# Strassen pairs of a conv-FFN: tokens normalized ahead of the split, four products in one PSUM bank, squares added in pairs

## The chip, the cores and the metric

The kernel runs on one core of a Trainium2 chip. The metric is the time of one execution in device microseconds. The core has a matrix engine (TensorE, PE), which multiplies a 128 x 128 stationary tile by a moving tile and writes to PSUM, and three engines for elementwise work: VectorE (DVE), ScalarE (ACT) and GpSimd (POOL). SyncE (SP) issues the DMAs. Each engine has its own list of instructions; semaphores join them.

## What is computed

One layer of a streaming encoder for 2080 tokens of width 1024 (2048 of a prompt, 32 of a running stream), in float32. The core of the reference:

```python
def rmsnorm(x, g):
    y = x32 * lax.rsqrt(jnp.mean(x32 * x32, axis=-1, keepdims=True) + NORM_EPS)
    return (y * g.astype(jnp.float32)).astype(x.dtype)

def conv_ffn(h, conv_prev, p):
    gu = h @ p['w_up']
    gate, up = gu[..., :D_FF], gu[..., D_FF:]
    gate_c, conv_new = causal_dwconv(gate, conv_prev, p['ffn_conv_w'], p['ffn_conv_b'])
    act = jax.nn.gelu(gate_c, approximate=True) * up
    return act @ p['w_down'], conv_new

def layer(x, ...):
    m, ... = mixer(rmsnorm(x, p['g_mix_pre']), ...)
    x = x + rmsnorm(m, p['g_mix_post'])
    f, ffn_conv_new = conv_ffn(rmsnorm(x, p['g_ffn_pre']), ffn_conv_prev, p)
    x = x + rmsnorm(f, p['g_ffn_post'])
```

The mixer is stick-breaking attention beside a state-space scan, with one input and one output projection. D_FF is 2816, so w_up makes 22 tiles of gate and 22 of up, each of 128 columns.

## The kernel before

**Layout.** Activations lie with features on the partitions and tokens along the free axis. The tokens are taken in four blocks s = 0 to 3 of 512, 512, 512 and 544. Every float32 factor is split into a high part (a copy rounded to float32r, made by ACT) and a low part (the rest, a subtract on POOL or DVE), and each product of tiles is three matmuls: high x high, high x low, low x high (`dense`, L145). So `part` (L1052) and `divide` (L130) are the split of an activation and of a weight tile.

**Order.** A first phase makes projections and the scan for all blocks. Then `build` runs attention for block s+1 (`Attention.heads`) with the rest of block s as its filler (`Tail.stream`, L1365): a Python generator whose steps `heads` draws between attention's own slots. For block 3 no attention is left; its stream runs alone, after `alone` (L1430) has given it more PSUM banks and more places for weights. The order in which the generators emit is the starting point; a planner that simulates time (`schedule_with_timeline_sim=True`) sets each engine's list from it, with one exception: `pin` (L69) ties the first matmul of a unit to the last one marked before, so that in blocks 0 to 2 PE keeps the emitted order of units, attention's scores and transposes among them. In block 3 pinning is off.

**The stream of a block** takes its tokens in two halves, a and b. `owed` is what is left of the block before: its last two downs, of which 8 steps go first. Then come

1. `out_units` of half a: the output projection, eight units of 24 matmuls;
2. `out_units` of half b, with `residual` and `ready` of half a emitted between its steps;
3. `residual` of half b;
4. in blocks 1 to 3 `squares`, `far`, the rest of `owed`, the root of half b, and two early pairs;
5. the pairs (or, in block 0, `up`), in groups of three or two, with `finish` of the block before and `down` of the last group between them.

`residual` (L991) makes h = x + rmsnorm(m): the root of mean squares of m by `rstd_narrow`, a multiply (L1010), the add (L1015, DVE and POOL in turn), a store of h (`hS`), and in blocks 1 to 3 the multiply by the gain (L1018, ACT), into m. `squares` (L1058) then squares h in place, which has to wait for the store.

`rstd_steps` (L182) is the root: matmuls with a column of ones (L193) sum the squares over the partitions, one output column for 128 tokens, one for each tile in `sq`, eight tiles in `root` (L1041); then a multiply-add on DVE, a power on POOL, and a matmul with the identity (L228) that spreads the result over the partitions as r.

**Strassen.** Blocks 1 to 3 compute gate and up of both token halves in seven products in place of eight (the Winograd form). `near` (L1062) splits half a, `far` (L1071) splits half b and makes three sums of tiles with their splits (`put`), X[6], X[7] and X[4]; `self.X` names the seven activations. Weight sums were made by block 0 and lie in DRAM (`sS`). The tokens are split **without** their root r: `pair` (L1142) multiplies the gate by r as it evicts it (L1180 on DVE, L1184 on POOL), and up stays unscaled, since the norm behind the down removes a scale of each token; `rcol` keeps what this does to its epsilon.

A pair (a gate tile and an up tile) is seven products of 12 matmuls of 256 columns (272 in block 3). Four PSUM banks are used: 1 and then 2 in one, 5 and 3, 6 and 7, and 4. Each bank is read where its first product is complete:

```python
        for i in (1, 2, 5, 6, 3, 7, 4) if j < AHEAD else (1, 5, 6, 2, 3, 7, 4):
            w = self.factor(s, j, i)
            base = {2: 1, 3: 5, 7: 6}.get(i, i)
            if base == i:
                ps[i] = self.bank()
```

ACT copies 1 (L1174) and 5 (L1176); DVE evicts 6, 3, 7 and 4 with an add (L1157) and 2 with r (L1180). Then follow the convolution over tokens (L1201, L1203), GELU (L1207 to L1210), the product with up (L1211), and the split into `ah` and `al` (L1216, L1217), which `down` (L1292) multiplies. The first two pairs (`AHEAD`) are early: their products 1 and 2 need half a only.

`factor` (L1115) fetches a weight: 1, 2 and 4 come split from DRAM (`wS_up`), the others come whole (`sS`, four `wraw` buffers) and are split by ACT (L135) and POOL (L136). In block 3 `slot` turns through ten places; elsewhere a ring of six (`w`) serves pairs and downs. `bank` turns through three banks (five in block 3). `finish` (L1330) is the last norm of the block before, its residual add and the store of y.

Of the kernel before, what the change touches and what calls it, by code (L numbers as in the profile page):

```python
# [20 lines left out]
RBUFS = 4  # L21
FAST = (1, 2, 3)
AHEAD = 2

# [38 lines left out]
class Kernel:  # L63
# [54 lines left out]
    def held(self, pool, tag):  # L118

        return pool.tile([P, 2, self.unit, P], F32R, name=tag or "w", bufs=1 if tag else self.wbufs)  # L120
# [810 lines left out]
class Tail:  # L931
# [7 lines left out]
    def __init__(self, kn, att, ctx, pu):  # L939
# [14 lines left out]
        self.raws, self.n, self.n_bank = {}, 0, 0  # L954
# [36 lines left out]
    def residual(self, s, half):  # L991
# [8 lines left out]
        self.h = []  # L1000
        for c in range(KC):
            m = self.m(c, half)
            if self.late:
                x = self.late.tile([P, 272], F32, name="xr", bufs=8)[:, :n]
            else:
                if c % 2 == 0:
                    pair = self.yp.tile([P, 548], F32, name="gb") if c % 4 else self.yp.tile([P, 546], F32, name="y")
                x = pair[:, 272 * (c % 2) : 272 * (c % 2) + n]
# [5 lines left out]
            h = x if fast else m  # L1014
            eng.tensor_tensor(h, m, x, op=ALU.add)  # L1015
            nc.sync.dma_start(kn.hS[s][:, c, c0:c1], h)
            if fast:
                nc.scalar.activation(m, h, AF.Copy, scale=kn.col(C_GFFN + c))  # L1018
            else:
                nc.scalar.activation(x, m, AF.Square)  # L1020
            self.h.append(x)
            yield

# [17 lines left out]
    def root(self, s, half, pin=False):  # L1041
        kn, nc, att = self.kn, self.kn.nc, self.att
        c0, c1 = half
        if c0 == 0:
# [4 lines left out]
            att.tmp, *kn.bank, self.h, c1 - c0, D, out=self.r[:, c0:c1], rcol=col, pin=pin  # L1049
# [8 lines left out]
    def squares(self):  # L1058
        for h in self.h:
            self.kn.nc.scalar.activation(h, h, AF.Square)  # L1060

    def near(self, s, half):  # L1062

        kn, nc = self.kn, self.kn.nc
        c0, c1 = half
        hi, lo = self.x = self.cat
        for k in range(KC):
            self.part(self.m(k, half), hi[k][:, c0:c1], lo[k][:, c0:c1], nc.vector if k % 2 else None)
            yield

    def far(self, s, half):  # L1071
# [24 lines left out]
        for k in two:  # L1096
            sub(b21, b22, b21, k)
# [17 lines left out]
    def factor(self, s, j, i):  # L1115


        kn = self.kn
        if i in (1, 2, 4):
            key = ("up", NJ + j if i == 4 else j, 4 * (i > 1))  # L1120
            return kn.recall(self.ring(), [key], 4, self.slot())
        return kn.divide(self.ring(), kn.raw(self.raws[j, i][:], 4), 4, None, self.slot())

    def ring(self):

        return self.keep or self.kn.wp

    def slot(self):

        if not self.keep:  # L1130
            return None
        self.n += 1
        return f"w{self.n % 10 // 2}{self.n % 2 * 4}"

    def bank(self):

        self.n_bank += 1
        k = max(self.n_bank, 0) % (5 if self.keep else 3)
        pool, name = self.pu if k >= (3 if self.keep else 2) else self.po
        return pool.tile([P, 512], F32, name=name)  # L1140

    def pair(self, s, j, acts):  # L1142
# [16 lines left out]
        for i in (1, 2, 5, 6, 3, 7, 4) if j < AHEAD else (1, 5, 6, 2, 3, 7, 4):  # L1159
            w = self.factor(s, j, i)  # L1160
            base = {2: 1, 3: 5, 7: 6}.get(i, i)
            if base == i:
                ps[i] = self.bank()
            b = ps[base]
            for k in (0, 2):
                kn.dense(
                    b, w[k : k + 2], self.X[i], 0, h, k0=k, first=base == i and k == 0, last=base != i and k == 2,
# [9 lines left out]
            elif i == 6:  # L1177
                add(t, b, p1)
            elif i == 2:
                nc.vector.tensor_tensor(gb[:, 2 : 2 + h], b, self.r[:, :h], op=ALU.mult)  # L1180
# [406 lines left out]
```

## Time and profile before

| | |
|---|---|
| median of 3 runs | 2983.7 us (2981.67 to 2986.89) |
| profiled execution | 2982.5 us |
| its span, first to last instruction | 2980.7 us |
| mean granted TensorE clock | 0.969 |
| DMA | 632.97 MB, mean 212 GB/s |

How to read the rows: in a row of instructions stand line, engine, operation, output<-inputs, the shape, the count, then busy time in us, mean ns of one, and the idle time of the engine just before them with what ended most of it. In a row by windows stand the window, its width, the busy time of PE, PE's weight loads, DVE, ACT and POOL (counts in brackets), the granted clock, the share of the DMA engines and GB/s. In a row of waits stand who waited, for whom, us in total, times, and the longest. In a timeline row stand start, duration, engine, line, operation and count, with idle time and its releaser in square brackets. A float32 matmul of one column is recorded as two. Tile names: `o`, `u`, `t` are PSUM banks, `n` the quarters of the tokens and their sums, `gb`, `y`, `ub` and `xr` work tiles.

### The profile page before, as it was taken

The page shows a single profiled execution, that of the slowest core. Times are in us where ns is not written, and L with a number is a line of the kernel's source. Part 1 is how long each engine was busy: PE and PEld are TensorE (multiplying, and loading weights), DVE is VectorE, ACT ScalarE, POOL GpSimd, SP SyncE. Part 2 cuts the span into 40 slices and gives each one's busy share as a digit, 9 for nine tenths or more (in the row PEclk, how much of TensorE's full clock was granted, in tenths as well). Part 3 has the DMA queues.
Part 4 walks back from the last instruction along what each step waited for, and adds up shares of the span by engine and source line. Part 5 has one row for each costly group of instructions (what it writes and reads, how often), then busy time and mean ns, then how long its engine had stood idle before and what let it go on. Part 6 is the DMA issues. An engine that isn't in the chain of part 4 may idle for free. (4 is left out here: it accounts for less than half of the span.)

```text
span 2980.7 us, 51672 instructions
## 1 busy us (share of the span) xinstructions
PE 2791.3 (94%) x18307; PEld 2485.9 (83%) x18307; DVE 1947.4 (65%) x2920; ACT 1464.4 (49%) x3075; POOL 1770.3 (59%) x1552
## 2 busy tenths in 40 slices
PE   7999999989899999999899999998999999789997
PEld 6777778877787778778788999987998989789997
DVE  7666576557675667746867667688577763744554
ACT  4344444337655445446655555666455544433322
POOL 4555565435756666645866666577666655855645
PEclk9999999989999999999899999999999999899998
DMA  5646463658687778786576667756666666666664
GB/s 177 181 152 174 149 177 122 160 150 286 230 273 262 263 268 284 273 285 230 168 242 206 213 214 244 265 166 209 214 209 209 206 229 213 210 205 210 203 222 140
DMA packets 371139, 632.97 MB, mean 212 GB/s; under 512 B 77531, under 2 KB 196963, under 8 KB 370883
## 3 DMA queue, kind: packets, MB, share of 16 engines
q1 hardware_dynamic: 370882, 629.67, 65.1%
q8 instruction: 146, 2.39, 0.3%
q14 instruction: 111, 0.90, 0.1%
HBM read 480.31 MB, written 149.23 MB: 211 GB/s over the span
## 5 line engine op out<-in xcount | busy, mean ns | idle before, releaser
L136 POOL TENSOR_TENSOR w<-wraw,w 128x512 fp32r<-128x512 f32 (+3 forms) x508 | 768.1, 1520 | 401.3 <-ACT w L135 372.4
L151 PE MATMUL o<-xhi,w 128*128 128x256 f32 (+2 forms) x3776 | 923.1, 328 | 28.8 <-ACT xhi L324 8.0
L151 PEld LDWEIGHTS o<-xhi,w 128*128 128x128 f32 x3776 | 653.8, 193 | 95.3 <-ACT xhi L324 8.0
L151 PE MATMUL o<-xlo,w 128*128 128x256 f32 (+2 forms) x1888 | 617.6, 327 | 5.9 <-DVE xlo L310 3.6
L135 ACT CAST w<-wraw 128x512 fp32r<-128x512 f32 (+3 forms) x508 | 335.0, 663 | 314.9 <-PE o L151 136.6
L709 POOL TENSOR_TENSOR beta<-beta,prow 128x512 f32<-128x512 f32 (+3 forms) x256 | 261.8, 1024 | 233.0 <-DVE prow L704 202.3
L151 PEld LDWEIGHTS o<-xlo,w 128*128 128x128 f32 x1888 | 364.6, 193 | 36.5 <-DVE xlo L310 5.3
L151 PE MATMUL o<-ah,w 128*128 128x512 f32 x992 | 345.4, 404 | 9.2 <-ACT ah L1287 4.3
L704 DVE TENSOR_TENSOR_SCAN prow<-gam,prow,z 128x513 f32<-128x513 f32 x192 | 244.8, 1276 | 31.0 <-ACT beta L702 29.2
L877 DVE TENSOR_TENSOR wt<-pt,wt 128x512 fp32r<-128x512 f32 (+2 forms) x320 | 190.3, 598 | 83.6 <-ACT wt L876 82.9
L151 PEld LDWEIGHTS o<-ah,w 128*128 128x128 f32 x992 | 187.2, 189 | 53.6 <-DVE f L1318 5.4
L151 PE MATMUL u<-xhi,w 128*128 128x256 f32 (+1 forms) x800 | 208.3, 337 | 6.7 <-DVE y L1282 6.6
L151 PE MATMUL o<-al,w 128*128 128x512 f32 x496 | 196.9, 397 | 0.3 <-POOL al L1217 0.3
L701 ACT ACTIVATE gam<-z 128x512 f32<-128x512 f32 (+2 forms) x320 | 173.4, 542 | 46.9 <-PE z L853 26.2
L876 ACT CAST wt<-pt 128x512 fp32r<-128x512 f32 (+2 forms) x320 | 167.0, 526 | 58.5 <-PE pt L872 56.5
L151 PE MATMUL o<-n,w 128*128 128x256 f32 (+1 forms) x1404 | 190.3, 285 | 4.3 <-DVE y L1157 2.5
L894 PE MATMUL pa<-wt,v 128*64 128x256 f32 (+3 forms) x1152 | 177.8, 283 | 16.4 <-DVE wt L877 9.7
L1203 DVE SCALAR_TENSOR_TENSOR y<-gb,cv,y 128x512 f32<-128x512 f32 (+1 forms) x132 | 169.7, 1285 | 27.3 <-ACT y L1201 20.4
L151 PEld LDWEIGHTS o<-n,w 128*128 128x128 f32 x1404 | 179.0, 190 | 6.0 <-DVE y L1157 2.8
L872 PE MATMUL pt<-ident,beta 128*128 128x128 f32 x1088 | 180.8, 278 | 1.9 <-POOL beta L709 1.1
L151 PE MATMUL t<-ah,w 128*128 128x272 f32 (+1 forms) x768 | 163.9, 303 | 14.5 <-ACT ah L1216 9.9
L894 PEld LDWEIGHTS pa<-wt,v 128*64 128x64 f32 (+1 forms) x1152 | 149.8, 166 | 31.5 <-DVE wt L877 12.3
(321 smaller groups left out, 6010.2 us busy)
## 6 DMA issues: line engine op xcount, KB each, us to landing
w<-wS_up SPq DMA_DIRECT2D x198, 512.0 KB, 3.9
wraw<-sS SPq DMA_DIRECT2D x264, 256.0 KB, 2.9
w<-wS_dn SPq DMA_DIRECT2D x144, 384.0 KB, 4.1
w<-wS_out SPq DMA_DIRECT2D x78, 512.0 KB, 5.8
wS_up<-w SPq DMA_DIRECT2D x66, 512.0 KB, 3.5
wraw<-wup SPq DMA_DIRECT2D x88, 256.0 KB, 3.9
sS<-wraw SPq DMA_DIRECT2D x88, 256.0 KB, 3.1
k<-kS SPq DMA_DIRECT2D x80, 256.0 KB, 4.0
```

The costliest lines, as they stand in the source:

```text
L135: nc.scalar.copy(hi, raw[:, :m, :])
L136: nc.gpsimd.tensor_tensor(lo, raw[:, :m, :], hi.bitcast(F32), op=ALU.subtract)
L151: mm = nc.tensor.matmul(ps[:, : c1 - c0], l, r, start=first and i == 0 and k == 0, stop=last and i == 2 and k == len(w) - 1, **({"skip_gro ...
L701: nc.scalar.activation(g[:, c0:512], z, AF.Sigmoid, scale=-0.125)
L704: nc.vector.tensor_tensor_scan(back(pr), back(g), z[:, 0:1].to_broadcast([P, n + 1]), self.kn.ones[:, 0:1] if prev is None else prev, op0= ...
L709: eng.tensor_tensor(b[:, :n], b[:, :n], pr[:, c0 + 1 : 513], op=ALU.mult)
L872: mm = nc.tensor.transpose(t[:, P * j : P * j + P], w[:, P * j : P * j + P], kn.ident[:])
L876: nc.scalar.copy(hi, t)
L877: nc.vector.tensor_tensor(lo, t, hi.bitcast(F32), op=ALU.subtract)
L894: nc.tensor.matmul(av[:m, 2 * P * p + c0 : 2 * P * p + 2 * P], v[:, j, :m], wt[:, rest, j, c0:], start=kc == s and p + j + rest == 0, stop ...
L1203: nc.vector.scalar_tensor_tensor(y[:, :W], gb[:, i : i + W], kn.col(wc + i), y[:, :W], op0=ALU.mult, op1=ALU.add)
```

## The change

- **Squares.** `residual` squares h at once, in blocks 1 to 3 into m, so that h itself stays. Two tiles' squares lie side by side, and pairs of tiles are added (POOL; the last of half b on DVE in blocks 1 to 3), so that the root multiplies two tiles by ones, not eight.
- **Normalized ahead of split and sums.** In blocks 1 to 3 `near` and `far` take the root first and multiply h by gain and r in one step (`scale`), r staying in PSUM. The pairs no longer multiply by r, and `rcol` falls away there. For half b the order is: residual, 20 owed steps, the root's first matmuls, four owed steps, its second ones, `far`.
- **Pairs.** In pairs that aren't early, products 1, 6, 7 and 4 are summed in one bank, 5 and 3 in another, 2 alone; ACT copies 6, 7 and 4, and DVE adds to 2 and 3. The order becomes 1, 5, 6, 2, 7, 3, 4. A table (`BANKS`) says which pool each bank is from.
- **Block 3.** The down of a group comes after the second pair of the next group. Acts lie in six places that take turns with output weights; the pairs' weights use the ring `w` and four places. 
- **Room.** A fifth `wraw` buffer; `rstd` of `finish` lies in `fsq`; a smaller DMA scratch.

```diff
-RBUFS = 4
+RBUFS = 5
+OWED = 20
+BANKS = (
+    ({1: 0, 5: 0, 2: 1}, {1: 1, 5: 0, 2: 0}, {1: 0, 5: 0, 6: 0, 4: 1}),
+    ({1: 1, 5: 0, 2: 0}, {1: 1, 5: 0, 2: 0}, {1: 0, 5: 0, 6: 1, 4: 1}),
+)
...
-            h = x if fast else m
+            h, sq = (x, m) if fast else (m, x)
             eng.tensor_tensor(h, m, x, op=ALU.add)
             nc.sync.dma_start(kn.hS[s][:, c, c0:c1], h)
-            if fast:
-                nc.scalar.activation(m, h, AF.Copy, scale=kn.col(C_GFFN + c))
-            else:
-                nc.scalar.activation(x, m, AF.Square)
-            self.h.append(x)
+            nc.scalar.activation(sq, h, AF.Square)
+            self.h.append(h)
+            if c % 2:
+                k = c % 4 - 1
+                two.append(
+                    self.Q[int(c0 > 0)][c // 4][:, k : k + 2, :n] if fast
+                    else pair[:, : 2 * n].rearrange("p (k t) -> p k t", k=2)
+                )
+                if c > 1:
+                    eng = nc.vector if fast and c0 and c == KC - 1 else nc.gpsimd
+                    eng.tensor_tensor(two[0], two[0], two[-1], op=ALU.add)
             yield
+        self.sq = [two[0][:, k, :] for k in range(2)]
...
+    def scale(self, half, k, r):
+        m = self.m(k, half)
+        self.kn.nc.vector.scalar_tensor_tensor(
+            m, self.h[k], self.kn.col(C_GFFN + k), r[:, : half[1] - half[0]], op0=ALU.mult, op1=ALU.mult
+        )
+        return m
...
     def near(self, s, half):
+        r = kn.rstd_narrow(att.tmp, *kn.bank, self.sq, c1 - c0, D, stay=True)
+        yield
         for k in range(KC):
-            self.part(self.m(k, half), hi[k][:, c0:c1], lo[k][:, c0:c1], nc.vector if k % 2 else None)
+            self.part(self.scale(half, k, r), hi[k][:, c0:c1], lo[k][:, c0:c1])
             yield
-    def far(self, s, half):
+    def far(self, s, half, r):
-        for k in two:
-            sub(b12, b12, b11, k)
         for k in range(KC):
-            self.part(self.m(k, half), hi[k][:, c0:c1], lo[k][:, c0:c1], nc.vector if k >= 4 else None)
+            m = self.scale(half, k, r)
+            if k in (1, 3):
+                sub(b12, b12, b11, two[k // 2])
+            elif k >= 4:
+                self.part(m, hi[k][:, c0:c1], lo[k][:, c0:c1], nc.vector if k % 2 else None)
+        for k in range(4):
+            self.part(self.m(k, half), hi[k][:, c0:c1], lo[k][:, c0:c1])
...
-            sub(b21, b22, b21, k)
+            sub(b21, b21, b22, k)
...
-        for i in (1, 2, 5, 6, 3, 7, 4) if j < AHEAD else (1, 5, 6, 2, 3, 7, 4):
+        early = j < AHEAD
+        onto = {2: 1, 3: 5, 7: 6} if early else {3: 5, 6: 1, 7: 1, 4: 1}
+        ends = {2, 3, 7, 4} if early else {2, 3, 4}
+        for i in (1, 2, 5, 6, 3, 7, 4) if early else (1, 5, 6, 2, 7, 3, 4):
...
             elif i == 6:
-                add(t, b, p1)
+                add(t, b, p1) if early else nc.scalar.copy(t, b)
             elif i == 2:
-                nc.vector.tensor_tensor(gb[:, 2 : 2 + h], b, self.r[:, :h], op=ALU.mult)
+                nc.scalar.copy(gb[:, 2 : 2 + h], b) if early else add(gb[:, 2 : 2 + h], b, p1)
             elif i == 3:
                 e = min(nt, 512) - h
-                add(t, b, t)
-                mul = lambda out, c: nc.gpsimd.tensor_tensor(out, t[:, c], self.r[:, h:nt][:, c], op=ALU.mult)
-                mul(gb[:, 2 + h : 2 + h + e], slice(0, e))
+                add(gb[:, 2 + h : 2 + h + e], b[:, :e], t[:, :e])
...
             elif i == 7:
-                add(u, b, p1)
+                add(u, b, p1) if early else nc.scalar.copy(u, b)
                 nc.gpsimd.tensor_tensor(v, v, u, op=ALU.add)
+            elif early:
+                add(u, u, b)
             else:
-                add(u, u, b, ALU.subtract)
+                nc.scalar.copy(u, b)
...
         if fast:
-            self.squares()
-            self.far(s, b)
+            yield from islice(owed, OWED)
+            root = kn.rstd_steps(att.tmp, *kn.bank, self.sq, b[1] - b[0], D, stay=True, pin=self.pin)
+            next(root)
+            yield from islice(owed, 4)
+            self.far(s, b, next(root))
             yield from owed
-            root = self.root(s, b, pin=True)
-            next(root)
             acts = {0: []}
-            self.n_bank = -4
             early = [self.pair(s, j, acts[0]) for j in range(AHEAD)]
             for p in early:
                 yield from islice(p, 4)
-            next(root)
...
-                if j == j0 and g and (g < len(groups) - 1 or s == NSB - 1):
+                if j == j0 + bool(self.keep) and g and (g < len(groups) - 1 or s == NSB - 1):
                     yield from self.down(s, g - 1, acts.pop(g - 1), tiles)
...
-    nc = bacc.Bacc("TRN2", target_bir_lowering=False, num_devices=1, dynamic_dma_scratch_size=1024)
+    nc = bacc.Bacc("TRN2", target_bir_lowering=False, num_devices=1, dynamic_dma_scratch_size=256)
```

More of the change, by code (lines that the diff above doesn't have):

```diff
@@ L1039, in split, with root @@
             yield
-    def root(self, s, half, pin=False):
+    def root(self, s, half):
         kn, nc, att = self.kn, self.kn.nc, self.att
@@ L1166, in pair @@
                 kn.dense(
[L1167 removed]
+                    b, w[k : k + 2], self.X[i], 0, h, k0=k, first=base == i and k == 0, last=i in ends and k == 2,
                     pin=self.pin, loose=True,
@@ L1338, in finish @@
         else:
-            out = {"out": att.tmp.tile([P, 272], F32, name="rstd")}
+            out = {"out": self.fsq[:, c0:c1]}
         for r in kn.rstd_steps(att.tmp, *kn.bank, sq, n, D, of=self.cols.pop((s, c0), None), **out):
@@ L1342, in finish @@
         for c in range(KC):
-            h = (self.late or att.tmp).tile([P, 272], F32, name="xr", bufs=8 if self.late else 2)
-            nc.sync.dma_start(h[:, :n], kn.hS[s][:, c, c0:c1])
+            if not self.late:
+                h = att.tmp.tile([P, 272], F32, name="xr", bufs=2)[:, :n]
+            else:
+                if c % 2 == 0:
+                    pair = self.late.tile([P, 548], F32, name="xr", bufs=4)
+                h = pair[:, n * (c % 2) : n * (c % 2) + n]
+            nc.sync.dma_start(h, kn.hS[s][:, c, c0:c1])
             nc.vector.scalar_tensor_tensor(
@@ L1362, in ready @@
             yield from self.split(s, half)
-        yield from self.root(s, half)
+            yield from self.root(s, half)
     def stream(self, s, cat):
-        nt = SBS[s][1]
+        kn, att, nt = self.kn, self.att, SBS[s][1]
         a, b = (0, nt // 2), (nt // 2, nt)
```

70 lines of the change are left out of this document (36 added, 34 removed).

## The prediction

> **What bounds the kernel now.** I read the head of the page first, then the busy times by stage, then what TensorE waited for.
>
> ```profile
> span 2980.7 us, 51672 instructions
> PE 2791.3 (94%) x18307; PEld 2485.9 (83%) x18307; DVE 1947.4 (65%) x2920; ACT 1464.4 (49%) x3075; POOL 1770.3 (59%) x1552
> ```
>
> TensorE (PE) sets the time, and the other four have room on average. The average hides stages. In the view by windows, the first figure after the width is PE's busy time:
>
> ```profile
> 1375.00:1500.00 125.00, 109.16 (x723) 97.15 (x722) 109.31 (x154) 77.67 (x183) 91.88 (x92) 0.92 0.62 201
> 1500.00:1920.00 420.00, 416.67 (x2973) 384.23 (x2972) 285.68 (x403) 228.66 (x499) 257.94 (x240) 1.00 0.70 230
> 1960.00:2060.00 100.00, 87.81 (x601) 81.14 (x600) 86.75 (x122) 66.39 (x151) 79.29 (x72) 0.90 0.55 181
> 2060.00:2440.00 380.00, 375.88 (x2644) 344.68 (x2643) 277.65 (x371) 212.75 (x449) 238.91 (x210) 1.00 0.64 206
> 2540.00:2625.00 85.00, 65.11 (x477) 63.02 (x477) 57.09 (x78) 33.45 (x71) 69.65 (x61) 0.90 0.66 216
> 2625.00:2940.00 315.00, 295.84 (x2292) 292.54 (x2290) 155.64 (x259) 106.06 (x213) 178.64 (x155) 0.98 0.60 190
> ```
>
> Rows 2 and 4 are the pairs of blocks 1 and 2, with attention beside them: PE is 99% busy, so nothing done there on other engines can pay. Rows 1, 3 and 5 are the changeovers of blocks 1, 2 and 3 (residual, split, sums, first pairs). PE idles 15.8 + 12.2 + 19.9 = 47.9 us there, and in the first VectorE (DVE, third figure) is at 109.3 of 125. Row 6 is the pairs and downs of block 3, which has no attention beside it: 19.2 us idle. The waits of PE name the releasers, first from 2540 to 2625, then from 2625 to 2930:
>
> ```profile
> PE t L151 <- ACT ub L1176: 6.4, 1, 6.4
> PE t L151 <- ACT y L1174: 3.4, 1, 3.4
> PE t L151 <- DVE gb L1180: 2.7, 1, 2.7
> PE o L151 <- ACT y L1174: 0.5, 1, 0.5
> ...
> PE t L151 <- ACT ah L1216: 3.5, 1, 3.5
> PE o L151 <- DVE gb L1180: 3.2, 2, 2.0
> PE t L151 <- ACT y L1174: 2.7, 1, 2.7
> ```
>
> **Part 1: squares in pairs, fewer matmuls for the root.** Today the root multiplies eight tiles of squares by a column of ones. These are its matmuls, the last row being the 16-token rest of block 3:
>
> ```profile
> L193 PE MATMUL u<-ones,gb 128*128 128x1 f32 x96 | 15.3, 254 | 0.0
> L193 PE MATMUL u<-ones,y 128*128 128x1 f32 x96 | 14.7, 245 | 0.0
> L193 PE MATMUL u<-ones,xr 128*128 128x1 f32 x64 | 7.8, 239 | 0.0
> L193 PE MATMUL u<-ones,xr 128*16 128x1 f32 x32 | 1.1, 164 | 0.0
> ```
>
> That is 256 + 32. Two summed tiles in place of eight leave a quarter, so 192 + 24 go. They overlap, so I price by the distance of starts, from the timeline of block 1:
>
> ```profile
> 1409.70 0.58 PE L193 MATMUL u<-ones,gb 128*128 128x1 f32 x4
> 1410.15 0.58 PE L193 MATMUL u<-ones,y 128*128 128x1 f32 x4
> ```
>
> Four take 0.45 us, 0.11 each: 192 x 0.11 = 21 us, and about 1 for the short ones (at most 0.11 each). **-22 us** (by the busy times above, three quarters of 38.9, at most 29; nothing where PE would wait anyway). 5.3 of it is in block 0, whose root keeps its place and has 48 fewer.
>
> These blocks also cost clock. Three of them, at 1407-1412, 1971-1974 and 2506-2509, are each followed by a stretch in which PE is counted fully busy and yet gets a lower clock (next to last figures but two):
>
> ```profile
> 1410.00:1415.00 5.00, 5.00 (x30) 5.00 (x30) 5.00 (x7) 2.54 (x6) 5.00 (x5) 0.63 0.18 56
> 1415.00:1420.00 5.00, 5.00 (x29) 4.51 (x28) 5.00 (x5) 4.55 (x11) 5.00 (x5) 0.69 0.36 105
> 1974.50:1978.00 3.50, 3.50 (x17) 3.26 (x17) 3.50 (x5) 2.52 (x7) 3.50 (x3) 0.52 0.00 0
> 2510.00:2514.00 4.00, 4.00 (x22) 4.00 (x21) 0.07 (x1) 1.24 (x3) 3.84 (x5) 0.57 0.94 277
> ```
>
> What is withheld is 5 x 0.37 + 5 x 0.31 + 3.5 x 0.48 + 4 x 0.43 = 6.8 us. A quarter of the one-column matmuls should mostly avoid it: **-5**, bounds 0 and -6.8. [...]
>
> **Part 2: normalized before the split.** The scale by the gain alone, 16 ScalarE (ACT) instructions per block, becomes 16 on DVE that also take r. Moved subtracts and sums have these rows:
>
> ```profile
> L1010 DVE SCALAR_TENSOR_TENSOR n<-n,cv,u 128x256 f32<-128x256 f32 x48 | 19.3, 474 | 7.4 <-PE u L228 7.4
> L1345 DVE SCALAR_TENSOR_TENSOR f<-f,cv,rstd 128x256 f32<-128x256 f32 x48 | 35.2, 801 | 0.8 <-ACT rstd L238 0.8
> L1056 DVE TENSOR_TENSOR xlo<-n,xhi 128x256 fp32r<-128x256 f32 x16 | 11.5, 731 | 3.3 <-ACT xhi L1055 3.3
> L1079 DVE TENSOR_TENSOR n<-n,n 128x512 f32<-128x512 f32 x16 | 17.1, 1097 | 0.0
> L1157 DVE TENSOR_TENSOR y<-o,y 128x256 f32<-128x256 f32 x60 | 24.8, 414 | 36.6 <-PE o L151 36.5
> L1210 POOL TENSOR_TENSOR y<-y,gb 128x512 f32<-128x512 f32 x44 | 57.9, 1316 | 62.6 <-ACT gb L1209 62.1 <-ACT wt L876 0.3
> ```
>
> The new scale reads r from PSUM as L1010 does, so 0.47 us is nearer than the 0.80 of L1345, whose r lies in SBUF. Per block DVE gains 16 x 0.47 = 7.6 and one pair sum (1.1), and loses six subtracts that go to GpSimd (POOL), 6 x 0.73 = 4.4, and one eviction of 0.41 in each early pair: +3.5 us. Five pair sums (1.3 each) and the six subtracts (about 0.9) put 12 us more on POOL. The half a part of this lies under the output projection of half b and I cost it at nothing; without that cover it would be its root chain, about 5 us a block by these two starts (ones to identity, the chain through DVE and POOL between them):
>
> ```profile
> 2519.43 0.36 PE L193 MATMUL u<-ones,sqt 128*128 128x1 f32 x2
> 2524.65 0.74 PE L228 MATMUL u<-ident,rn_v 128*128 128x128 f32 x6
> ```
>
> A product is 12 matmuls, which take 1.5 us at the spacing of the chain of waits' longest piece:
>
> ```profile
> 2833.64 22.54 PE t L151 x177
> ```
>
> For half b the chain becomes a wait: the far split now starts after r, not beside it. On DVE, what stands behind the scale are attention's scans and the evictions, for which PE waits; on PE, with its pinned order, attention's scores stand behind the identity matmul. The cover for the 5.2 us is four steps of the owed down, then products 1 and 2 of two pairs (48 matmuls, about 6 us); and product 2 needs the copy of 1, into a tile that the scale must first release. Then product 6 needs eight scales, four subtracts of 1.1 and a split. In blocks 1 and 2 the split gains 3.5 us on a DVE that is nearly full, and starts later, while PE arrives earlier by the roots it saved: **+2.5 each, +5**, bounds -5 and +10 each. In block 3 PE loses the 2.7 us wait for gb (DVE was in the split) and the squares no longer overwrite h, so they don't wait for its store; against that stand about 1.5 us of uncovered chain and some 2 of split: **0**, bounds -8 and +8.
>
> **Part 3: four products in one bank.** In a pair that isn't early, products 6, 7 and 4 are copied by ACT where DVE added, gate's multiply by r goes, from DVE and from POOL (0.75 of a POOL busy 178.6 of 315 in block 3). In blocks 1 and 2 PE is full: nothing. In block 3 the down comes a pair later, so that the pair's last tiles (ah) are ready: of the 3.5 + 3.2 + 2.7 us of waits shown and the low clock behind them (0.98 of 315 us, 6 us withheld) I take **-10**, bounds 0 and -16. The new wait: PE may not go on in the bank until ACT has copied it, three times a pair with one product (12 matmuls) between, where there were two. The copies themselves are short:
>
> ```profile
> L1176 ACT COPY ub<-t 128x272 f32<-128x272 f32 x14 | 5.4, 382 | 17.1 <-PE t L151 17.0
> 2580.26 0.65 ACT L1216 CAST ah<-y 128x544 fp32r<-128x544 f32 x1 [6.68 <-DVE y L1213]
> 2580.81 0.38 ACT L1176 COPY ub<-t 128x272 f32<-128x272 f32 x1
> ```
>
> 0.38 us fits well into 12 matmuls; but the last two rows show a copy that stood 6.7 us behind a cast that waited for DVE. In block 3 the 44 ACT copies of its 22 pairs cost PE 6.4 + 3.4 + 0.5 + 2.7 = 13.0 us, 0.30 each. I take **+4** for all 180 added copies (3 in each of 20 pairs of 3 blocks), since most of the 13 fell together with half finished tokens' DVE work; bounds 0 and 180 x 0.30 = 54. At the very end product 3 comes 12 matmuls (1.5 us) later than 7, less two multiplies on POOL of 1.1: **+0.4**.
>
> The fifth raw buffer, the shared slots, the smaller scratch and the layout of residual tiles issue no DMA more; SP's queue keeps its order but for the later down. 0; if prefetch got worse, the first place is block 3.
>
> **Sum**: -22 - 5 + 5 + 0 - 10 + 4 + 0.4 = -27.6. The profiled execution took 2982.5 us, 1.8 outside its span of 2980.7, and 1.2 under the median 2983.7. 2982.5 - 27.6 = **2955**.
>
> **Rivals.**
> B, the changeovers loosen more: squares free of the store and ACT free of 32 scalings speak for it, DVE's load against. A third of the 47.9 us idle (16) goes in place of +5: 2982.5 - 22 - 5 - 16 - 10 + 4 + 0.4 = 2934.
> C, the changeovers are DVE's: what PE saves there is waited for again, the clock's 5 too, only block 0's 5.3 us stay, and the longer split costs 5 a block in blocks 1 and 2: -5.3 + 10 - 10 + 4 + 0.4 = -1, 2982. For it: DVE at 109.3 of 125. Against: PE is full where half a's root and block 3's stand.
> D, **slower**: ACT holds the bank. Each added copy waits as those of block 3 did, 54 us: 2982.5 - 31.6 + 54 = 3005. It decides from 31.6 / 180 = 0.18 us a copy. For it: the 6.7 us row. Against: blocks 1 and 2 put attention between products. [...]
> E, the change hardly reaches the path: the planner issues the sums where PE would wait anyway: 2982.
>
> **Chances.** Forecast (2945 to 2972) 0.50, B 0.16, C 0.18, D 0.14, E 0.02. Within 0.2% (6 us, what a measurement can tell from no change) lie most of C and E, 0.15; slower D and the tail of C, 0.15; faster the rest, 0.70. The range, 2925 to 2992, takes in B, C and the milder half of D's bound, and leaves out about 0.17.
>
> **What would show it.** One-column matmuls in u: 72 in place of 288 of these, and no 0.6 clock behind them; rows 2 and 4 still 99% busy; PE waits for `n` or `xhi` in the changeovers above 8 us a block mean C; waits of PE for the ACT copies above 30 us in sum mean D; no wait for ah before 2930 but the last one means the later down works. I would be wrong most likely in the changeovers, whose order the planner makes anew.

## The result and the profile after

| | before | after |
|---|---|---|
| median on the same chip | 2985.3 us (2981.67 to 2994.65) | 2959.05 us (2955.23 to 2959.21) |
| ratio after / before | | 0.9904 [0.988, 0.9929] |
| span of the profiled execution | 2980.7 us | 2957.3 us |

The change makes the kernel 1.0% faster. The head of the page after, span and busy times:

```profile
span 2957.3 us, 51214 instructions
PE 2759.0 (93%) x18091; PEld 2455.2 (83%) x18091; DVE 1877.7 (63%) x2789; ACT 1503.6 (51%) x3207; POOL 1763.6 (60%) x1497
```

PE's busy time fell by 32.3 us, the span by 23.4. I cut both spans at the first multiply of the norm ahead of each block's output projection (L800 before, L810 after), so that one piece is the stream of one block. Before, the four streams take 539.0, 550.7, 592.2 and 522.0 us; after, 529.7, 565.0, 582.4 and 503.1 (the head before them 776.8 and 777.1). So block 0 gave 9.3 us and block 3 18.9, while blocks 1 and 2 together lost 4.5.

The view by windows of the kernel after, with its own changeovers of blocks 1, 2 and 3 (rows 1, 3, 5) and the pairs (rows 2, 4, 6):

```profile
1375.00:1500.00 125.00, 105.63 (x716) 92.76 (x715) 118.30 (x163) 84.31 (x192) 100.39 (x96) 0.96 0.61 195
1500.00:1860.00 360.00, 355.14 (x2490) 325.51 (x2489) 224.57 (x289) 210.67 (x467) 215.28 (x181) 1.00 0.67 216
1960.00:2060.00 100.00, 80.89 (x585) 73.08 (x584) 95.33 (x129) 69.03 (x153) 80.50 (x73) 0.97 0.53 165
2060.00:2440.00 380.00, 372.67 (x2622) 343.73 (x2623) 239.44 (x307) 221.78 (x489) 222.96 (x188) 0.99 0.67 221
2500.00:2600.00 100.00, 73.74 (x466) 67.39 (x466) 69.99 (x111) 41.10 (x92) 75.73 (x75) 0.85 0.64 202
2600.00:2907.00 307.00, 304.03 (x2420) 303.09 (x2419) 127.59 (x232) 131.72 (x290) 165.76 (x126) 1.00 0.70 220
```

The pairs of block 3 (last row) are now full: 3.0 us idle of 307, at the whole clock, where before 19.2 of 315 were idle. The changeovers did not gain: PE idles 19.4 us in the first (15.8 before), 19.1 in the second (12.2) and 26.3 in the third (16.3 from 2504.5 to 2604.5 before, the same place after the start of the block), and DVE is busy 118.3 of 125 in the first (109.3). What PE waited for from 2500 to 2600, and then from 2600 to 2907:

```profile
PE o L161 <- DVE y L1186: 7.4, 1, 7.4
PE o L161 <- DVE ub L1186: 7.1, 1, 7.1
PE u L203 <- POOL xlo L1073: 3.5, 1, 3.5
PE u L238 <- POOL rn_v L226: 3.2, 1, 3.2
PE u L203 <- DVE n L1037: 2.8, 1, 2.8
...
PE t L161 <- DVE f L1348: 1.6, 1, 1.6
PE o L161 <- ACT ub L1226: 0.9, 1, 0.9
PE o L161 <- ACT ub L1221: 0.5, 1, 0.5
```

L203 is the root's one-column matmul, L238 its identity, L1037 the sum of the squares, L1073 the low part in the split, L1186 an eviction with an add. The third to fifth row, 9.5 us, are the chain of block 3's half b, which stood beside the split before. The first two, 14.5 us, have another cause. In the timeline of DVE both evictions stand behind the eight multiplies of `finish` of block 2 (L1380):

```profile
2553.89 8.94 DVE L1380 SCALAR_TENSOR_TENSOR f<-f,cv,fsq 128x256 f32<-128x256 f32 x8
2564.29 0.43 DVE L1186 TENSOR_TENSOR y<-o,y 128x272 f32<-128x272 f32 x1
2575.86 7.88 DVE L1380 SCALAR_TENSOR_TENSOR f<-f,cv,fsq 128x256 f32<-128x256 f32 x8 [0.67 <-ACT fsq L248]
2586.96 0.43 DVE L1186 TENSOR_TENSOR ub<-o,y 128x272 f32<-128x272 f32 x1
```

PE goes on at 2564.9 and 2587.5, right behind them. Before, the wait of 6.4 us for `ub` had the same cause (the ACT cast ahead of that copy waited for DVE until 2580):

```profile
2570.00 7.92 DVE L1345 SCALAR_TENSOR_TENSOR f<-f,cv,rstd 128x256 f32<-128x256 f32 x8
```

From 2600 to 2907 no wait for the split acts is left (`ah` and `al` before; in the new places their tiles are called `w`, written at L1247 and L1248), and the waits for the copies of the shared bank (the last two rows) are small.

Next the one-column matmuls and the identity of half b of block 1 in the timeline after:

```profile
1403.60 1.00 PE L203 MATMUL u<-ones,n 128*128 128x1 f32 x8
1409.37 0.61 PE L238 MATMUL u<-ident,rn_v 128*128 128x128 f32 x4
```

And the stretch behind them by windows (the granted clock is the last figure but two):

```profile
1405.00:1410.00 5.00, 5.00 (x31) 4.12 (x30) 2.88 (x6) 3.43 (x7) 5.00 (x7) 1.00 0.07 23
1410.00:1415.00 5.00, 5.00 (x44) 5.00 (x44) 5.00 (x12) 4.95 (x17) 4.65 (x6) 1.00 0.52 179
```

Eight in place of 32, and 1.00 behind them where 0.63 and 0.69 stood. Both came as forecast. What they were worth is another question, and the experiments answer it differently. Over the whole profiled execution the mean granted clock is 0.969 in both kernels.

### The profile page after: what moved, and what is told of

The parts are those of the page before. It is cut to its first block, busy times and chain, and to the rows that moved or that the text cites. A ratio compares the mean times of both kernels' runs of the same rounds, so it can differ in the third digit from the quotient of the medians.

```text
span 2957.3 us, 51214 instructions
## 1 busy us (share of the span) xinstructions
PE 2759.0 (93%) x18091; PEld 2455.2 (83%) x18091; DVE 1877.7 (63%) x2789; ACT 1503.6 (51%) x3207; POOL 1763.6 (60%) x1497
## 4 chain that ended last, share of the span: by engine, by line
PE 36%; DVE 7%; DMA 3%; issue 2%; ACT 2%; POOL 1%; SPq 0%; DVEq 0%; ACTq 0%; POOLq 0%
PE o L161 18%; PE t L161 9%; PE u L161 3%; PE pa L904 2%; PE z L863 2%; PE pt L882 2%; DVE prow L714 2%; DVE f L1380 1%; DVE y L1235 1%; DMA w<-wS_out 1%; DVE wt L887 1%; POOL w L146 1%; DMA xr<-hS 1%; DVE f L1384 0%; DMA o_fconv<-gb 0%
## 5 line engine op out<-in xcount | busy, mean ns | idle before, releaser
L719 POOL TENSOR_TENSOR beta<-beta,prow 128x512 f32<-128x512 f32 (+3 forms) x256 | 271.4, 1061 | 225.1 <-DVE prow L714 203.0
L161 PE MATMUL o<-n,w 128*128 128x256 f32 (+1 forms) x1608 | 222.3, 287 | 9.9 <-DVE y L1186 7.4
L161 PEld LDWEIGHTS o<-n,w 128*128 128x128 f32 x1608 | 207.0, 190 | 12.8 <-issue 7.6
L161 PE MATMUL u<-xhi,w 128*128 128x512 f32 (+1 forms) x672 | 179.5, 343 | 6.8 <-DVE y L1313 4.7
L1235 DVE SCALAR_TENSOR_TENSOR y<-gb,cv,y 128x512 f32<-128x512 f32 (+1 forms) x132 | 147.4, 1117 | 50.6 <-ACT y L1233 48.2
L712 ACT ACTIVATE beta<-z 128x512 f32<-128x512 f32 (+2 forms) x320 | 172.9, 540 | 0.0
```

What stands on the lines that cost most here:

```text
L161: mm = nc.tensor.matmul(ps[:, : c1 - c0], l, r, start=first and i == 0 and k == 0, stop=last and i == 2 and k == len(w) - 1, **({"skip_gro ...
L712: nc.scalar.activation(b[:, :n], z, AF.Sigmoid, scale=0.125)
L719: eng.tensor_tensor(b[:, :n], b[:, :n], pr[:, c0 + 1 : 513], op=ALU.mult)
L1235: nc.vector.scalar_tensor_tensor(y[:, :W], gb[:, i : i + W], kn.col(wc + i), y[:, :W], op0=ALU.mult, op1=ALU.add)
```

## The experiments

Each kernel was timed against the kernel before on the same chip; a ratio is to that. Streams, stretches and waits are read from one profiled execution of each kernel, which took between 4 us less than its median (e11) and 16 us more (e9). The experiments on the change come first, then its parts put into the kernel before.

**e1: the change with four raw buffers.**

```diff
-RBUFS = 5
+RBUFS = 4
```

> The changed kernel with four raw weight buffers in place of five, nothing else. The prediction's theory (the fifth buffer is worth nothing): within 4 us of the changed kernel's 2959 us, and block 0's pairs of gate and up keep about 14 us of idle PE between the third GELU and the next block. Rival (block 0 gained from the fifth buffer, since there each raw buffer is held by the weight sums as well): 8 to 17 us slower, with SyncE waiting longer for raw buffers and PE idle back near 30 us in that stretch.

Measured: 2955.87 us, 0.9893 [0.9871, 0.9914], against 0.9904 for the change. No difference. On its own this would say that the buffer is worth nothing; e11 shows that in the kernel before it is worth 24 us.

**e2: the change with a root of eight tiles.**

```diff
-                if c > 1:
-                    eng = nc.vector if fast and c0 and c == KC - 1 else nc.gpsimd
-                    eng.tensor_tensor(two[0], two[0], two[-1], op=ALU.add)
-        self.sq = [two[0][:, k, :] for k in range(2)]
+        self.sq = [t[:, k, :] for t in two for k in range(2)]
```

> The changed kernel without the adds of pairs of squares: the root multiplies eight tiles by ones again, everything else as changed. The prediction's theory (the one-column matmuls are PE time on the path, and some clock behind them): 20 to 27 us slower than 2959. Rival C (PE waits in the changeovers anyway): at most 8 us slower, block 0's share. If the pair sums themselves are in the way (GpSimd is late with them), it could even be faster in blocks 1 to 3.

Measured: 2947.37 us, 0.9864 [0.9842, 0.9885]. Without the pair sums the kernel is faster, not slower. Block 0 takes 515.0 us in place of 529.7; the other streams stay within 4 us.

**e3: block 3's down where it was.**

```diff
-                if j == j0 + bool(self.keep) and g and (g < len(groups) - 1 or s == NSB - 1):
+                if j == j0 and g and (g < len(groups) - 1 or s == NSB - 1):
```

> The changed kernel with the down of block 3 directly after the first pair of the next group, as before the change. The prediction's theory (the later down clears the waits for ah and the banks in block 3): about 10 us slower, up to 16, all in block 3 after its third pair. Rival (the copies on ScalarE and less work on GpSimd cleared block 3): at most 3 us slower.

Measured: 2957.41 us, 0.9892 [0.9869, 0.9915]: the same. As a mark in block 3's pairs I take the start of the convolution (L1201 before), the step ahead of GELU. The stretch from the fourth to the last convolution takes 303.7 us, 300.1 in the change, 320.9 before, and in it PE waits for the high part of an act nowhere and once for a low part, 2.0 us. It was not the later down that removed that wait.

**e4: the change with the old four banks.**

```diff
-        onto = {2: 1, 3: 5, 7: 6} if early else {3: 5, 6: 1, 7: 1, 4: 1}
-        ends = {2, 3, 7, 4} if early else {2, 3, 4}
-        for i in (1, 2, 5, 6, 3, 7, 4) if early else (1, 5, 6, 2, 7, 3, 4):
+        onto = {2: 1, 3: 5, 7: 6}
+        ends = {2, 3, 7, 4}
+        for i in (1, 2, 5, 6, 3, 7, 4) if early else (1, 5, 6, 2, 3, 7, 4):
...
-                nc.scalar.copy(u, b)
+                add(u, u, b)
```

> The changed kernel with the old four banks for a pair that isn't early: order 1, 5, 6, 2, 3, 7, 4, products 6, 3, 7 and 4 added by VectorE, 2 copied by VectorE; normalized tokens, pair sums and the later down stay. The prediction's theory (the one bank brings nothing in blocks 1 and 2 and costs 4 us of ScalarE waits in all): 2955, between 4 us faster and 4 us slower than the changed kernel. Rival (the one bank with ScalarE's copies is what made block 3's pairs free of stalls, or unloaded VectorE in the changeovers): 8 to 20 us slower.

Measured: 2945.54 us, 0.9859 [0.9835, 0.9882]. One bank costs some 13 us, although its copies are hardly waited for. One place where it loses is the end of block 2's pairs. There PE's waits in the kernel after, from 2280 to 2450, have this row:

```profile
PE u L161 <- DMA w<-wS_up: 5.7, 1, 5.7
```

SyncE's timeline just before it:

```profile
2364.50 5.16 SPq L137 DMA_DIRECT2D w<-wS_out  x6
2370.68 0.32 SPq L122 DMA_DIRECT2D wraw<-sS  x1
2371.32 0.34 SPq L137 DMA_DIRECT2D w<-wS_up  x1
```

And the two windows around it:

```profile
2370.00:2380.00 10.00, 5.33 (x43) 4.91 (x41) 5.89 (x6) 5.13 (x12) 7.81 (x6) 0.95 1.03 411
2380.00:2390.00 10.00, 8.54 (x52) 8.37 (x53) 1.73 (x3) 3.99 (x9) 3.88 (x3) 0.71 1.05 387
```

Six loads of block 3's output weights were issued ahead of a weight of the running pair; the DMA engines are full, PE waits 5.7 us for that weight, and then runs at 0.71. Waits for `wS_up`, 3.4 us in sum in e2 and 5.7 to 8 in the others, stand in this place in all seven kernels with one bank (the change, e1, e2, e3, e5, e7, e8), and in none of e4, e6, e9 and e12, which have four. The four wait 2.3 to 3.0 us for `wS_out` there. So a part of the loss lies in an order of loads that came with the one bank, and not in the bank being held. The streams say roughly where the whole of it lies. Blocks 1 and 2 together take 8.1 us more in the change than in e4 (1147.4 and 1139.3), and 17.9 more in e5 than in e6 below (1154.9 and 1137.0); block 3 takes 1.6 more and 2.1 less. (e12, also with four banks, takes 1147.1 for blocks 1 and 2 in an execution 6 us over its median, so this is no close reading.) What else one bank slows there stays open.

**e5: pair sums in blocks 1 to 3 only. e6: the same, with the old banks as in e4.**

```diff
-                if c > 1:
+                if c > 1 and fast:
...
-        self.sq = [two[0][:, k, :] for k in range(2)]
+        self.sq = [t[:, k, :] for t in (two[:1] if fast else two) for k in range(2)]
```

> The changed kernel with pair sums in blocks 1 to 3 only; block 0's root multiplies eight tiles by ones again. Theory now (the run without any pair sums was faster by what they cost in block 0: 8 of 9.7 us less PE idle in its changeover, although PE has 5 us more to do there): block 0 from its first norm to block 1's takes 513 to 520 us in place of 530, the other blocks as in the changed kernel: 2942 to 2950. Rival (the sums cost in blocks 1 to 3, or the planner's new order made the difference by chance): 2955 to 2965.

> Pair sums in blocks 1 to 3 only, and the old four banks with VectorE's adds (the two edits that each ran faster than the changed kernel). If both causes are real and lie in different blocks they add: 2930 to 2938 us, a ratio to the kernel before of 0.980 to 0.984. If they are two draws of the planner's order: 2943 to 2960.

Measured: e5 2945.56 us, 0.9865 [0.9847, 0.9882], block 0 at 515.4; e6 **2931.31 us, 0.9827 [0.9808, 0.9847]**. So the sums in block 0 cost what e2 gained, the sums elsewhere are worth little, and the two edits add up. e6 beats both kernels. Its page:

```profile
span 2928.0 us, 51351 instructions
PE 2756.0 (94%) x18139; PEld 2458.3 (84%) x18139; DVE 1938.3 (66%) x2969; ACT 1453.9 (50%) x3027; POOL 1746.3 (60%) x1491
```

**e7: GpSimd multiplies given back to block 3** (by a tile of ones, in its pairs). **e8: the change with the old weight places, act buffers and raw buffers, and the early down.**

```diff
+                    add(t, b, t)
+                    mul = lambda out, c: nc.gpsimd.tensor_tensor(out, t[:, c], self.r[:, h:nt][:, c], op=ALU.mult)
+                    mul(gb[:, 2 + h : 2 + h + e], slice(0, e))
+                    mul(gb[:, 516:548], slice(e, h))
```

```diff
-        self.n_act += 1
-        a = self.keep.tile([P, 1088], F32R, name=ACTS[self.n_act % len(ACTS)])
-        return a[:, :544], a[:, 544:]
+        return self.gp.tile([P, 544], F32R, name="ah"), self.gp.tile([P, 544], F32R, name="al")
```

> The changed kernel with GpSimd's two multiplies per pair given back in block 3 (by a tile of ones): VectorE adds product 3 to t, GpSimd multiplies it into gb, 1.1 us a pair. Theory P (block 3's pairs were bound by GpSimd, 10.9 us of work against 10.6 of PE, and the multiply was the excess): 15 to 25 us slower, PE idle in block 3's pairs near 20 us in place of 4. Rival S (the new places for weights and acts cleared them): at most 4 us slower.

> The changed kernel with block 3's weights in the old ten places, acts in the old four buffers, four raw buffers and the down directly after the first pair, all as before the change; the multiply on GpSimd stays away. Rival S (the places cleared block 3's pairs): 15 to 25 us slower, all in block 3 after its third pair. Theory P (GpSimd's multiply did): at most 4 us slower. If both hold in part, each of this and of the run with the multiply shows 5 to 12.

Measured: e7 2968.73 us, 0.9949 [0.9929, 0.9969]; e8 2966.62 us, 0.9938 [0.9922, 0.9953]. From the fourth to the last convolution e7 takes 310.5 us and e8 310.7. The multiplies in e7, the groups of GpSimd from 2600 to 2910, and then the longest wait of PE in block 3's pairs, in e7 (2612 to 2924; L1253 writes the high part of an act) and in e8 (2618 to 2931):

```profile
L1217 POOL TENSOR_TENSOR gb<-y,r 128x240 f32<-128x240 f32 x18 | 13.5, 750 | 9.4 <-DVE y L1186 9.1
L1217 POOL TENSOR_TENSOR gb<-y,r 128x32 f32<-128x32 f32 x18 | 5.0, 275 | 0.0
```

```profile
PE t L161 <- ACT w L1253: 3.8, 1, 3.8
PE t L161 <- ACT ah L1243: 6.8, 5, 4.0
```

18.5 us of multiplies on a GpSimd that is not the bottleneck cost the kernel 10 us by the medians and 13 by the ratios; block 3's stream takes 516.3 us in place of 503.1. The wait for an act is back with them, in the new places. In e8 the longest of the five waits, 4.0 us at 2929.5, is that of the last down for the last pair, which the other kernels have too, behind their windows (6.3 before, 4.6 in the change); 2.9 us are left. So with either edit taken back PE waits for acts again in the change's pairs, and no run gives the gain to the buffers alone (e9, with multiplies, new places and four banks, has no such wait there). e8 costs 8 us by the medians and 10 by the ratios, but block 3's stream takes only 4.6 us more; blocks 0 and 1 take 5.9 and 8.1 more, and of its edits only the missing fifth raw buffer reaches them, which by itself cost 2.3 and 1.7 (e1).

**e9, e10 and e11 start from the kernel before.** e10 has the pair sums of blocks 1 to 3 alone, e11 the fifth raw buffer alone; e9 has both, with the new places, act buffers and later down, which is e6 without normalizing ahead.

```diff
+            if c % 2 and c > 1:
+                nc.gpsimd.tensor_tensor(two[0], two[0], two[c // 2], op=ALU.add)
+        self.h = self.h[:2]
```

```diff
-RBUFS = 4
+RBUFS = 5
...
-            out = {"out": att.tmp.tile([P, 272], F32, name="rstd")}
+            out = {"out": self.fsq[:, c0:c1]}
...
-dynamic_dma_scratch_size=1024)
+dynamic_dma_scratch_size=256)
```

> The kernel before with everything of e6 except the normalization ahead of the split: pair sums in blocks 1 to 3, fifth raw buffer, new places and act buffers, later down; the old banks, the old far with the root after it, and the products multiplied by the rstd on DVE and GpSimd as before. Against e6 (2931.3 us) it tells what the normalization is worth by itself. Theory: it is worth about 10 us in block 3 (e7: the GpSimd multiplies alone took the pairs from 300.1 to 310.5 us) and costs a few us in the changeovers of blocks 1 and 2 (the prediction had 2.5 each): 2934 to 2942 us, block 3's stream near 512 us, blocks 1 and 2 together 1130 to 1137. Rival one: the normalization is worth nothing, the places and act buffers gave block 3 its time: 2925 to 2932, block 3 near 502. Rival two: the old changeover is much worse than the new one: over 2945.

> The kernel before with the pair sums of the squares in blocks 1 to 3 alone. The prediction's first part at its own place: 17 us of one-column matmuls less in these blocks and 5 us less of withheld clock: 2963 to 2968 us, each of the three streams about 7 us shorter. Rival: as from e2 to e5, the sums are worth about 2 us in all, since the waits for the last squares and the adds take the place of the matmuls: 2980 to 2986 us.

> The kernel before with the fifth raw weight buffer alone (and the room that it takes: a smaller DMA scratch, finish's rstd in the place of its squares). Block 0 was 539.0 us before and 515 us in e2 and e5, which have its old root; the fifth buffer is the one other edit there. Theory: the buffer does it, through an earlier arrival of weights in the middle of block 0 (PE idle there 30.5 us before, 7 in e2 and e5): block 0 at 513 to 522 us and the kernel at 2962 to 2972 us. Rival: block 0 stays within 5 us of 539 and the kernel within 6 of before; what shortened block 0 is then another order of the whole plan, not the buffer.

Measured: e10 2986.75 us, 1.0001 [0.999, 1.0011]: the sums are worth nothing in the code of before. The head of e10's page has the matmuls saved:

```profile
PE 2777.9 (93%) x18139; PEld 2474.6 (83%) x18139; DVE 1951.5 (65%) x2920; ACT 1466.4 (49%) x3075; POOL 1792.5 (60%) x1570
```

PE's waits in e10 from 1930 to 2062, the changeover of block 2, have what came for them:

```profile
PE z L853 <- DVE prow L704: 6.3, 7, 1.9
PE pt L872 <- POOL xlo L1058: 3.4, 1, 3.4
PE pt L872 <- DMA wraw<-sS: 2.9, 1, 2.9
```

PE is busy 13.4 us less, and the span is 1.2 us longer (2981.9): PE came earlier and waited, for attention's scan on DVE (`prow`, 3.6 us in this stretch before), for the split on GpSimd (`xlo`), whose list now holds the sums as well, and for a weight. The low clock came all the same: the mean granted clock was 0.93 in the changeover of block 1 (1372 to 1500; 0.92 from 1375 to 1500 before), where the longest wait was 5.0 us, 0.95 in that of block 2 (0.92 from 1930 to 2060 before), and 0.966 in the whole profiled execution (0.969 before).

e11: 2962.15 us, **0.9912 [0.9895, 0.9928]**. The buffer alone gives 24 us by the medians, and block 0 takes 516.1 in place of 539.0, as its theory said. (The smaller scratch that makes room for it is no rival: e1 and e8 have that scratch with four buffers, and ACT's wait for raw w_up stays there at 52.1 us.) ACT's waits in the kernel before, from 860 to 1316, and then e11's from 855 to 1290:

```profile
ACT w L135 <- DMA wraw<-wup: 51.0, 34, 3.9
ACT w L135 <- DMA wraw<-wdn: 16.5, 17, 2.6
```

```profile
ACT w L135 <- DMA wraw<-wup: 14.4, 12, 2.2
```

L135 is the high part of a weight. What stands behind a wait in ACT's list came late in the prediction's rows: a copy at 2580.81 behind a cast that had waited 6.68 us for DVE. And what PE waited for in the same stretch of the kernel before were late evictions and splits:

```profile
PE u L151 <- DVE y L1282: 6.6, 5, 2.7
PE o L151 <- ACT ah L1287: 4.3, 3, 2.8
```

In e11 the first is 0.6 us and the second is gone. None of PE's rows names the raw buffer. That ACT's wait is what made these late is inferred from the lists; the experiment shows the buffer's effect on both.

e9: 2943.93 us, 0.9855 [0.9837, 0.9874], a little over the upper end of its theory, 2942. So normalizing ahead (e9 to e6) is worth 8 us by the ratios (0.0028 x 2986), 13 by the medians; the intervals just overlap. The step holds all that goes with it: the new changeover and, in the pairs, the multiplies by r that fall away. Block 3's stream, 506.3 us, lies between the 512 and the 502 of the two theories; its stretch from the fourth to the last convolution is already at 302.2 us in e9 and 296.9 in e6. (These two figures of e9 come from its execution of 2959.77 us, 16 over its median.)

**e12: e4 with block 0's sums on DVE.**

```diff
-                    eng = nc.vector if fast and c0 and c == KC - 1 else nc.gpsimd
+                    eng = nc.vector if not fast or c0 and c == KC - 1 else nc.gpsimd
```

> e4 (the change with the old four banks, 2945.5 us, block 0 at 526.9) with the six adds of the squares' pairs in block 0 on DVE in place of GpSimd. It asks why the sums cost block 0 some 12 to 14 us (e6, which has none there: 2931.3 us, block 0 at 514.8). Theory: GpSimd is the loaded engine there, and adds of 1.3 to 1.7 us each in its queue delay the low parts of the weights, so that raw buffers come free later (ACT waits 31.7 us for raw w_up in e4, 12.8 in e6): with the adds on DVE block 0 takes 512 to 519 us, ACT's wait for raw w_up falls under 20 us, and the kernel takes 2927 to 2935 us. Rival: the adds cost as much on any engine, since the root waits for the last of them and the work behind is planned in another order: block 0 at 524 to 531 us and the kernel at 2942 to 2950.

Measured: 2942.42 us, 0.9848 [0.9825, 0.9871]; block 0 at 521.7 us, ACT's wait for raw w_up 23.5. That lies between the two theories. ACT's wait falls by 8 of the 19 us that the sums added (31.7 in e4, 12.8 in e6), so GpSimd's load seems to be a part of it; but the 5 us in block 0 are no more than streams of identical code differ by, and the intervals of e12 and e4 overlap.

Block 0 in all kernels, with ACT's wait for raw w_up (from 860 to 1300):

| | raw buffers | sums in block 0 | ACT's wait, us | block 0, us |
|---|---|---|---|---|
| e6, e9, e5, e11, e2 | 5 | none | 12.8, 13.1, 13.8, 14.4, 14.7 | 514.8, 520.2, 515.4, 516.1, 515.0 |
| e12 | 5 | on DVE | 23.5 | 521.7 |
| e4, e7, e3, after | 5 | on GpSimd | 31.7, 33.4, 36.7, 37.8 | 526.9, 527.7, 530.0, 529.7 |
| e1, e8 | 4 | on GpSimd | 52.1, 52.1 | 532.0, 535.6 |
| before, e10 | 4 | none | 51.0, 54.4 | 539.0, 541.3 |

Between the groups with five buffers the wait and the time go together; with four the wait is long with and without sums. With four buffers block 0 is 3 to 9 us shorter with the sums, which agrees with the prediction's 5.3; with five the sums on GpSimd cost 7 to 15.

## Why the prediction was right, and where it was not

2955 was forecast and 2959 measured, inside the range. That is luck: the terms did not come as they were worked out, and large misses of both signs cancelled. A path from before to after in steps (ratios x 2986; by the intervals the first is uncertain by 5 us, each other by 7 to 9). Taken in another order the steps differ: the fifth buffer, first here, was worth nothing when taken last (e1).

| step | to ratio | worth |
|---|---|---|
| fifth raw buffer (e11) | 0.9912 | -26 |
| places, act buffers, later down, and the sums of blocks 1 to 3 (e9) | 0.9855 | -17 |
| normalized ahead (e6) | 0.9827 | -8 |
| one bank (e5) | 0.9865 | +11 |
| sums in block 0 (after) | 0.9904 | +12 |

- **Part 1, -22 and -5: failed.** The count was right (72 of these matmuls in place of 288, and no 0.6 clock behind the roots of blocks 1 and 2; of the six roots before, three had shown it). But 17 of the 22 us, and the clock, lie where rival C put them: what PE saves there is waited for again. e10 measures 0 for them (1.0001), and so does e2 against e5 in the changed code (0.9864 and 0.9865). The step that failed is "nothing where PE would wait anyway", which I wrote down and then did not subtract. In block 0 the 5.3 us agree with the streams as long as there are four raw buffers; with five they turn into about +12.
- **Fifth raw buffer, 0: failed, and the largest miss.** I judged it by the DMAs that it adds, none, and looked at block 3. Its place was block 0, where ACT's waits for raw weights, 67.5 us in 456, were in the trace of before. I had read PE's waits only, which name DVE and ACT.
- **Part 2, +5 and 0: not refuted, and not measured alone.** Normalizing ahead gained about 8 us from e9 to e6, at the edge of what the intervals tell, but that step also holds the multiplies that fall away, which I had counted in part 3; what is left for the changeovers is lost in the intervals. The place was foreseen: the changeovers of blocks 1 and 2 idle 3.5 and 6.9 us more than before. For block 3 the stretch up to its fourth convolution took 153.0 us, 150.9 before, and 0 was forecast; that `finish` holds DVE there was not in my sum. One reading was wrong: the 0.80 us of L1345 is a mean of instructions of 471 to 1520 ns with a median of 478, so it doesn't show that an r in SBUF is slower. The new scale took 0.47, as forecast.
- **Part 3, block 3, -10: right in kind, about half in size.** Block 3's stream fell by 18.9, its stretch from the fourth to the last convolution by 20.8. The reason given, the later down, is wrong: e3 is the same without it. Two other edits did it, the places with the act buffers and the gone multiplies, which I had given no price of their own on a GpSimd busy 178.6 of 315. Their gains overlap: with the multiplies kept, the new places bring block 3's stream to 506.3 us (e9; 524.4 in e11, without them), and with the old places the gone multiplies bring it to 507.7 (e8). In the change the multiplies are worth 10 to 13 (e7). The places and the act buffers were not separated.
- **Part 3, one bank, +4: mis-sized, 11 to 14** (0.0038 x 2986 from e6 to e5, 0.0045 x 2986 from e4 to the change). Rival D's mechanism fell: PE's waits for the added copies are 4.1 us in the whole of the change, not 54. What the traces show in its place is the wait of 5.7 us for a weight with 2.9 withheld behind it (10 x 0.29), where the four-bank kernels wait 2.3 to 3.0. The rest lies, as far as streams tell, in blocks 1 and 2 and not in block 3, and is open. My price of a copy was off as well: 6.4 of the 13.0 us in it had DVE's multiplies of `finish` behind them.
- **The end, +0.4: right.** From the last convolution to the end 50.0 us, 50.2 before.

Open: why six adds of tiles in block 0 hold up the raw weights, beyond what GpSimd's load explains; whether normalizing ahead would pay without the new places, which no run tried; and the fifth buffer's gain of zero in the changed code (e1) is measured but follows from no step here, except that its wait there falls only from 52.1 to 37.8.

## What to carry to other kernels

Before pricing a buffer, ask which engine waits for what lies in it, over all engines' lists of waits, and not only for the one that sets the time: in block 0 PE's rows named DVE and ACT (6.6 and 4.3 us), and the wait for the raw weights (67.5 us) stood in ACT's list. Matmuls taken away from stages in which PE also waits were worth nothing here (e10: 13.4 us less busy, ratio 1.0001); take such a stage's idle time off the gain first. Look also at what stood ahead of a wait's releaser in its engine's list: behind the longest waits for evictions and copies in block 3 (7.4 and 7.1 us, 6.4 before) were a norm's multiplies on DVE. And split a change that mixes edits: here two of its five steps cost 23 us together, and leaving them out (e6) nearly doubled the gain.

## What the runs showed of the hardware

- Eight one-column matmuls left the granted clock at 1.00 in the change (1405 to 1415), where 32 of them were followed by 0.63 and 0.69 before (1410 to 1420), with PE busy 5.00 of 5 us there and in the 5 us ahead. But it is no rule: three of the six such groups before were followed by 1.00 (1372 to 1380, 1924.5 to 1930 and 2542 to 2546). The low clock also stood behind gaps: in the change 0.71 from 2380 to 2390, behind a wait of 5.7 us, and 0.50 from 1425 to 1430, behind 5 us in which PE was busy 2.76. That is no rule either: before, PE was busy 1.26 of 4 us from 2546 to 2550 and had 1.00 in the next 4.
- The DMA engines were full for 20 us in a kernel whose mean is 214 GB/s: 411 and 387 GB/s at a share of 1.03 and 1.05 from 2370 to 2390. The weight issued at 2371.3 landed at 2380.9, 9.6 us later; one issued at 2355.7 had taken 3.4.
- Streams of identical code differ by some 5 us from run to run: block 0 takes 514.8 to 520.2 us in the five kernels of the table's first row, and the head before it 774.3 in e6 and 778.8 in e5 (block 1 starts at 1289.1 and 1294.2). Gains below that can only be read from ratios of several executions, not from one trace.
